# Multi-query attention: a planned schedule gets a second open accumulation group, a delay for dependent VectorE steps, longer lag and filler matmuls

## The chip, the cores and the metric

The kernel runs on one core of a Trainium2 chip. The metric is device time in microseconds (us) of that core. "Before" and "changed" are timed in alternating rounds on the same chip. Ratios are the mean time of one kernel's fast runs over that of the other's fast runs of the same rounds, so they are not quite the ratio of the medians quoted.

Names: TensorE (PE in the profile) multiplies matrices, ScalarE (ACT) computes the exponentials, VectorE (DVE) does elementwise work, SP issues transfers.

## The reference

```python
# q: (8, 1024, 16, 64), k and v: (8, 1024, 64), float32; one k and v for all 16 heads
scores  = np.matmul(q, k.T) / np.sqrt(64)        # per batch and head
weights = np.exp(scores - max); weights /= weights.sum(-1)
out     = np.matmul(weights, v)                  # (8, 1024, 16, 64)
```

## The kernel before

Two heads form a pair; there are 64 pairs, each with 8 tiles of 128 keys. For each tile TensorE computes scores in two halves ("qk", two matmuls each), and the exponential of a half goes to ScalarE ("act"). 77 of the 512 tiles are not exponentiated by ScalarE: VectorE copies their scores out ("z", twice) and makes the exponential from six elementwise steps. Then TensorE adds the weights up over the 8 tiles of a pair in three groups ("av"): group 0 sums the rows (weights of ones, 32 columns each), groups 1 and 2 multiply with v. VectorE evacuates each group ("ev"); a transposing transfer and a normalisation ("rec", "norm") follow.

The order of all this is not left to a scheduler. A function `plan` simulates TensorE, ScalarE and VectorE with fixed durations and writes a list of operations; each engine then executes its part of the list strictly in that order, waiting where data is not there yet.

```python
ACT_P, ACT_L = 0.905, 1.19                     # the plan's durations, us
QK_P, AV_P, SWITCH, PE_L = 0.22, 0.217, 0.10, 0.49
VEC = dict(z=1.13, ev=0.6, rec=0.22, norm=1.13)
STEPS = (0.6, 0.6, 0.6, 1.13, 1.13, 1.13)
TURN = 9.0                                     # evacuation to normalisation
BACKLOG, WBUFS, LAG = 4.5, 22, 1.4             # (three lines in the kernel)

def plan(NP, NKT):
    ...
    p, g, left = 0, 0, set(range(NKT))         # the one open group: pair, group, tiles left
    while p < NP:
        if pe <= dve:                          # TensorE's next operation
            ...
            # VectorE takes a tile where its work in hand is below BACKLOG
            if not vunits and nt < NT - NKT and todo < BACKLOG: ...
            ...                                # rs[j]: when tile j of the open group is ready
            j = min(rs, key=lambda j: (rs[j], j))
            tav = max(rs[j], acc[nacc % 2] if len(left) == NKT else 0.0)
            lag = min(LAG, 0.35 + (2 * NT - nq) / (6 * NKT))
            av = tav <= T + (SWITCH if mode != "av" else 0) and (
                nv < 3 * NKT * (nq / (2 * NKT) - lag) or nq == 2 * NT)
            ...
        else:                                  # VectorE's next operation, in this preference:
            ...                                # z, ev, rec/norm, then the steps of the oldest tile
            elif steps:
                t, n = steps.pop(0)
                emit(T, "step", t, n)
                dve = T + STEPS[n]
```

The lag keeps the value work some pairs behind the scores, so that TensorE has a stock of it; it shrinks towards the end. In the changed kernel `BACKLOG`, `WBUFS` and `LAG` become 5.0, 28 and 1.8.

The softmax here doesn't subtract the row's maximum and nothing guards it: scores larger than these inputs give would overflow.

## Time and profile before

| | before |
|---|---|
| time, median of 5 runs | 835.91 us (835.71 to 839.54) |
| span of the profiled run | 833.3 us |
| first exponential starts / last one starts | 9.19 / 818.57 us |
| median distance of two exponentials' starts | 904 ns |
| sum of the 869 distances above 904 ns ("excess") | 23.8 us |
| last exponential's start to the end ("tail") | 14.7 us |
| half-clock stretches before the last exponential | 9, together 51.2 us |

The excess, worked out from the instruction records: ScalarE is the fullest engine, it needs 904 ns per exponential, and what the distances add above that is time lost. Start + 869 x 904 ns + excess + tail gives the span.

The page of the kernel before: the span, each engine's busy time, the granted TensorE clock in 40 slices (tenths of full speed), and two groups by line with count, busy time, mean duration and the idle time before them.

```profile
span 833.3 us, 15240 instructions
...
PE 760.8 (91%) x6172; PEld 238.5 (29%) x6172; DVE 796.5 (96%) x943; ACT 803.1 (96%) x873; POOL 76.4 (9%) x91
...
PEclk8898999899999999999999999999999999999989
...
L339 ACT ACTIVATE wt<-sc 128x1024 f16<-128x1024 f32 x870 | 800.7, 1230 | 9.7 <-PE sc L327 9.6
L327 PE MATMUL sc<-qt,k2t 64*128 64x512 f16 x2048 | 364.1, 393 | 50.8 <-ACT wt L339 40.2
```

Two engines are 96% busy, and several slices show a clock of 8 tenths. The waits of the kernel before (who waited for whom, us in total, times, longest):

```profile
PE sc L327 <- ACT wt L339: 40.2, 112, 0.5
...
ACT wt L339 <- PE sc L327: 9.6, 20, 0.9
...
PE acc L383 <- DVE wt L370: 7.8, 24, 0.8
...
PE sc L327 <- DVE z L350: 4.7, 8, 1.1
```

The first wait is harmless: scores are ahead of ScalarE. The other three are not: ScalarE waits for scores, TensorE waits for a finished VectorE tile, and TensorE waits for VectorE to empty a score buffer. The TensorE timeline of the kernel before, ahead of the half-clock stretch at 236.7 us (start, duration, what, number of matmuls, idle time before and its releaser):

```profile
232.98 0.40 PE L383 MATMUL acc<-wt,ones 128*32 128x512 f16 x4
233.31 0.39 PE L327 MATMUL sc<-qt,k2t 64*128 64x512 f16 x2
234.13 0.39 PE L327 MATMUL sc<-qt,k2t 64*128 64x512 f16 x2 [0.43 <-ACT wt L339]
235.05 0.39 PE L327 MATMUL sc<-qt,k2t 64*128 64x512 f16 x2 [0.52 <-ACT wt L339]
236.37 1.18 PE L327 MATMUL sc<-qt,k2t 64*128 64x512 f16 x6 [0.92 <-DVE z L350]
237.50 0.62 PE L383 MATMUL acc<-wt,ones 128*32 128x512 f16 x4
```

From 233.3 to 237.5 us TensorE has score work only, though it has value work of later groups to do: the one open group lacks a tile that VectorE is still making. VectorE's last step of that tile:

```profile
236.23 1.22 DVE L370 TENSOR_TENSOR wt<-z,g 128x2048 uint16<-128x2048 uint16 x1
```

It ends at about 237.45 us, and the row-sum step that reads the tile starts at 237.50. The group of four row-sum matmuls takes 0.40 us at 232.98 and 0.62 us at 237.50: the clock has halved in between (the clock records show 0.50 for 3.4 us from 236.70 us).

### The profile page before, as it was taken

What the parts mean: (1) busy time and instruction counts of PE and PEld (TensorE: products, weight loads), DVE (VectorE), ACT (ScalarE), POOL (GpSimd) and SP (SyncE); (2) the same over time, 40 slices, a digit from 0 to 9 for tenths busy, and PEclk for the clock granted to TensorE, in tenths of its full rate; (3) what the DMA queues carried; (4) which work ended last, traced back from release to release, by engine and by line L of the source; (5) the groups of instructions that cost most, each with busy time, mean ns of one, the idle gap of its engine ahead of it and who ended that gap; (6) DMA issues with size and microseconds to landing.
All of it is one profiled execution on the core that took longest, in us unless ns stands there. A gap on an engine that the chain in (4) does not pass through costs nothing. (4 is left out here: it accounts for less than half of the span.)

```text
span 833.3 us, 15240 instructions
## 1 busy us (share of the span) xinstructions
PE 760.8 (91%) x6172; PEld 238.5 (29%) x6172; DVE 796.5 (96%) x943; ACT 803.1 (96%) x873; POOL 76.4 (9%) x91
## 2 busy tenths in 40 slices
PE   4988999899989989989989989999999999999986
PEld 1222232223323323323323323323323323323322
DVE  6999999999999999999999999999999999999994
ACT  6999999999999999999999999999999999999993
POOL 5100011010110002000020000000001000000000
PEclk8898999899999999999999999999999999999989
DMA  9956697667986689776698686775787676764524
GB/s 151 94 97 106 117 148 115 117 106 117 153 133 97 119 121 136 125 132 92 117 155 106 122 137 109 123 127 96 126 138 108 122 125 99 127 112 87 101 70 114
DMA packets 329846, 97.86 MB, mean 117 GB/s; under 512 B 263216, under 2 KB 329776, under 8 KB 329776
## 3 DMA queue, kind: packets, MB, share of 16 engines
q1 hardware_dynamic: 239792, 76.70, 47.1%
q0 software_dynamic: 88400, 19.40, 26.3%
q8 instruction: 48, 0.79, 0.4%
q10 hardware_dynamic: 1584, 0.79, 0.3%
q14 instruction: 22, 0.18, 0.1%
HBM read 39.58 MB, written 33.55 MB: 88 GB/s over the span
## 5 line engine op out<-in xcount | busy, mean ns | idle before, releaser
L339 ACT ACTIVATE wt<-sc 128x1024 f16<-128x1024 f32 x870 | 800.7, 1230 | 9.7 <-PE sc L327 9.6
L327 PE MATMUL sc<-qt,k2t 64*128 64x512 f16 x2048 | 364.1, 393 | 50.8 <-ACT wt L339 40.2
L391 PE MATMUL acc<-wt,v 128*64 128x512 f16 x2048 | 304.5, 393 | 0.0
L350 DVE TENSOR_SCALAR z<-sc 128x1024 uint16<-128x1024 f32 x154 | 187.6, 1218 | 10.2 <-PE sc L327 9.1
L327 PEld LDWEIGHTS <-k2t 64*128 64x128 f16 x2048 | 102.7, 94 | 323.2 <-issue 314.5
L383 PE MATMUL acc<-wt,ones 128*32 128x512 f16 x2048 | 167.7, 390 | 7.8 <-DVE wt L370 7.8
L399 DVE CAST ots<-acc 128x512 f16<-128x512 f32 x192 | 130.5, 679 | 10.2 <-PE acc L391 8.6
L391 PEld LDWEIGHTS <-v 128*64 128x64 f16 x2048 | 90.7, 109 | 152.9 <-issue 120.6
L275 POOL DMA_DIRECT2D qn<-in_q_dram x63 | 56.4, 895 | 638.0 <-DMA qt<-qn 637.6
L370 DVE TENSOR_TENSOR wt<-z,g 128x2048 uint16<-128x2048 uint16 x77 | 93.8, 1218 | 1.3 <-ACT wt L339 0.5
L369 DVE TENSOR_TENSOR g<-m,g 128x2048 f16<-128x2048 f16 x77 | 93.9, 1219 | 1.2
L368 DVE TENSOR_TENSOR m<-f,m 128x2048 f16<-128x2048 uint16 x77 | 93.7, 1217 | 0.0
L421 DVE TENSOR_TENSOR osb<-otq,rec 128x1024 f32<-128x1024 f16 x63 | 76.9, 1221 | 1.4
L383 PEld LDWEIGHTS <-ones 128*32 128x32 f16 x2048 | 42.8, 94 | 103.9 <-issue 96.7
L364 DVE TENSOR_SCALAR m<-f 128x2048 f16<-128x2048 uint16 x77 | 54.2, 704 | 2.2
L366 DVE TENSOR_SCALAR g<-f 128x2048 f16<-128x2048 uint16 x77 | 53.0, 689 | 0.0
L362 DVE TENSOR_SCALAR f<-z 128x2048 uint16<-128x2048 uint16 x77 | 52.8, 686 | 0.2
L412 DVE RECIPROCAL rec<-otq 128x16 f32<-128x16 f16 x63 | 15.3, 243 | 0.0
L253 POOL DMA_DIRECT2D k<-in_k_dram x14 | 12.5, 897 | 10.9 <-DMA k2t<-k 10.1
L260 POOL DMA_DIRECT2D v<-in_v_dram x8 | 7.0, 880 | 8.4 <-PE acc L391 7.3
L315 PE MATMUL kps<-ident,k 128*128 128x128 f16 x8 | 1.0, 308 | 5.9 <-DVE k L304 5.9
L320 ACT COPY qt<-qps 128x512 f16<-128x512 f16 x2 | 1.2, 586 | 4.8 <-PE qps L318 4.8
(18 smaller groups left out, 10.8 us busy)
## 6 DMA issues: line engine op xcount, KB each, us to landing
out_dram<-osb SPq DMA_DIRECT2D x63, 512.0 KB, 4.1
qn<-in_q_dram POOLq DMA_DIRECT2D x63, 256.0 KB, 4.6
k<-in_k_dram POOLq DMA_DIRECT2D x14, 128.0 KB, 5.5
v<-in_v_dram POOLq DMA_DIRECT2D x8, 128.0 KB, 6.2
qt<-qn SPq DMA_TRANSPOSE x63, 3.1
otq<-ots SPq DMA_TRANSPOSE x63, 4.8
qf<-in_q_dram ACTq DMA_DIRECT2D x2, 256.0 KB, 4.5
kn<-in_k_dram SPq DMA_DIRECT2D x1, 256.0 KB, 4.1
```

Source lines behind the costliest of these rows:

```text
L275: nc.gpsimd.dma_start(out=qn[p], in_=q[b, :, 2 * hp : 2 * hp + 2, :].rearrange("(c p) h d -> p c (h d)", p=P),)
L327: nc.tensor.matmul(sc[t, c][:, h, :], kst[p // HP]["k2t"][64 * h : 64 * h + 64, j, :], qt[p].rearrange("p c x -> p (c x)")[64 * h : 64 * h ...
L339: nc.scalar.activation(out=wt[t][:, :, c * QC : (c + 1) * QC], in_=sc.pop((t, c)), func=EXP, scale=ascale)
L350: nc.vector.tensor_scalar(out=z[:, :, c * QC : (c + 1) * QC], in0=sc.pop((t, c)), scalar1=vscale, scalar2=15 * ONE, op0=ALU.mult, op1=ALU.add,
L364: lambda: V.tensor_scalar(out=m, in0=f, scalar1=-ONE, scalar2=1.0 / ONE, op0=ALU.add, op1=ALU.mult),
L368: lambda: V.tensor_tensor(out=m, in0=f, in1=m, op=ALU.mult),
L369: lambda: V.tensor_tensor(out=g, in0=m, in1=g, op=ALU.mult),
L370: lambda: V.tensor_tensor(out=w.bitcast(U16), in0=z, in1=g, op=ALU.add),
L383: nc.tensor.matmul(a[32 * g : 32 * g + 32, :], ones16, w[:, h, cq * QC : (cq + 1) * QC], start=(n == 0), stop=(n == NKT - 1), tile_positio ...
L391: nc.tensor.matmul(a[64 * h : 64 * h + 64, :], vt[:, j, :], w[:, h, cq * QC : (cq + 1) * QC], start=(n == 0), stop=(n == NKT - 1), tile_po ...
L399: nc.vector.tensor_copy(out=ots[p][:, grp, :], in_=acc.pop((p, grp)))
L421: nc.vector.tensor_tensor(out=osb.rearrange("p i (h d) -> p (i h) d", h=2), in0=otq.pop(p)[:, 4:12, :].rearrange("p i (h d) -> p (i h) d", ...
```

## The change

Its intent, as far as the diff shows it: keep TensorE supplied, so that neither it nor its clock ever falls behind ScalarE. The core of the diff:

```diff
+VEC_DEP = 0.12
-BACKLOG = 4.5
-WBUFS = 22
-LAG = 1.4
+BACKLOG = 5.0
+WBUFS = 28
+LAG = 1.8
+def follows(x, y):     # does VectorE operation x read what y has just written?
...
-    while p < NP:
+    while p < NP or groups:
...
+            while len(groups) < 2 and p < NP:          # two open groups
+                a = 0 if all(x[3] for x in groups) else 1
+                groups.append((p, g, set(range(NKT)), a))
...              # the tile that is ready first, of the older group where one is ready
-            e = [x for x in evs if x[0] <= T]
-            f = [x for x in fin if x[0] <= T]
+            todo = [("ev", x) for x in evs if x[0] <= T]
+            todo += [("fin", x) for x in fin if x[0] <= T][:1]
+            todo += [("step", x) for x in steps if ...][:2]   # steps of two tiles
+            free = [x for x in todo if not follows(x[1], last)]
+            late = VEC_DEP if not free else 0.0
+            what, x = (free or todo or [("", None)])[0]
...
+        if len(run) >= 20 and True:                    # long runs of scores get fillers
+            idle.update(run[:-1])
...
+        for _ in range(10):                            # before the first transposes
+            for g in range(4):
+                nc.tensor.matmul(cold[32 * g : 32 * g + 32, :], ones16, wide, ...)
         turn_first()
...
+                if i in idle:
+                    fill(args[0] // NKT, 1)            # four matmuls into a free bank
```

`VEC_DEP` is what the trace of the kernel before shows: a VectorE step that reads what the step just before it wrote starts 1249 ns after that step, an independent one 1133 ns (719 against 600 ns for the shorter steps).

Besides, VectorE's buffer `g` is dropped (the weights tile holds that value) and `z` gets a third buffer, the first loads share the output buffers' pool, v is loaded two pairs later, and pair 62 is normalised ahead of the last evacuation instead of at the very end.

More of the change, by code (lines that the diff above doesn't have):

```diff
@@ L32 @@
 VEC_L = 0.19
+VEC_DEP = 0.12
 TURN = 9.0
-BACKLOG = 4.5
-WBUFS = 22
-LAG = 1.4
+BACKLOG = 5.0
+WBUFS = 28
+LAG = 1.8
 FAR = 1e9
+def follows(x, y):
+    if y is None or len(x) != len(y) and y[0] != "z":
+        return False
+    if len(x) == 3:
+        return x[1] == "norm" and y[1] == "rec" and x[2] == y[2]
+    if len(x) != 2:
+        return False
+    if y[0] == "z":
+        return x == (y[1], 0)
+    return x[0] == y[0] and (x[1], y[1]) in ((1, 0), (2, 0), (3, 1), (4, 3), (5, 4))
 def plan(NP, NKT):
@@ L54, in plan @@
     acc = [0.0] * 2
-    nacc = nq = nv = 0
+    nq = nv = 0
     nt, units, vunits = 0, [], []
@@ L61, in plan @@
     used = [0] * NT
-    p, g, left = 0, 0, set(range(NKT))
+    p, g = 0, 0
+    groups: list = []
     zs: list = []
@@ L66, in plan @@
     steps: list = []
-    while p < NP:
+    last = None
+    while p < NP or groups:
         if pe <= dve:
@@ L89, in plan @@
                 kind = "act"
-            rs = {}
-            for j in left:
-                t = NKT * p + j
-                if t in vtiles:
-                    rs[j] = ready.get(t, FAR)
-                elif g == 0:
-                    rs[j] = max(ready.get((t, 0), FAR), ready.get((t, 1), FAR))
-                else:
-                    rs[j] = ready.get((t, g - 1), FAR)
-            j = min(rs, key=lambda j: (rs[j], j))
-            tav = max(rs[j], acc[nacc % 2] if len(left) == NKT else 0.0)
+            while len(groups) < 2 and p < NP:
+                a = 0 if all(x[3] for x in groups) else 1
+                groups.append((p, g, set(range(NKT)), a))
+                g = (g + 1) % 3
+                p += g == 0
+            tav, pick = FAR, None
+            for grp in groups:
+                gp, gg, left, a = grp
+                for j in left:
+                    t = NKT * gp + j
+                    if t in vtiles:
+                        r = ready.get(t, FAR)
+                    elif gg == 0:
+                        r = max(ready.get((t, 0), FAR), ready.get((t, 1), FAR))
+                    else:
+                        r = ready.get((t, gg - 1), FAR)
+                    if len(left) == NKT:
+                        r = max(r, acc[a])
+                    if r < tav and (tav > T or grp is groups[0]):
+                        tav, pick = r, (grp, j)
             lag = min(LAG, 0.35 + (2 * NT - nq) / (6 * NKT))
@@ L139, in plan @@
                 nv += 1
-                emit(st, "av", p, g, j, NKT - len(left), nacc % 2)
-                left.discard(j)
-                used[NKT * p + j] += 1
-                if not left:
-                    acc[nacc % 2] = FAR
-                    evs.append((st + PE_L, p, g, nacc % 2))
-                    nacc += 1
-                    left = set(range(NKT))
-                    g = (g + 1) % 3
-                    p += g == 0
+                grp, j = pick
+                gp, gg, left, a = grp
+                emit(st, "av", gp, gg, j, NKT - len(left), a)
+                left.remove(j)
+                used[NKT * gp + j] += 1
+                if not left:
+                    acc[a] = FAR
+                    evs.append((st + PE_L, gp, gg, a))
+                    groups.remove(grp)
             else:
@@ L155, in plan @@
             z = [x for x in zs if x[0] <= T + 0.25]
-            e = [x for x in evs if x[0] <= T]
-            f = [x for x in fin if x[0] <= T]
+            todo = [("ev", x) for x in evs if x[0] <= T]
+            todo += [("fin", x) for x in fin if x[0] <= T][:1]
+            todo += [("step", x) for x in steps if x == min(y for y in steps if y[0] == x[0])][:2]
+            free = [x for x in todo if not follows(x[1], last)]
+            late = VEC_DEP if not free else 0.0
+            what, x = (free or todo or [("", None)])[0]
             if z:
-                zs.remove(z[0])
-                r, s, u = z[0]
+                x = z[0]
+                zs.remove(x)
+                r, s, u = x
                 T = max(T, r)
@@ L166, in plan @@
                     steps += [(u[0], n) for n in range(len(STEPS))]
-            elif e:
-                evs.remove(e[0])
-                _, ep, eg, a = e[0]
+                last = ("z", u[0])
+            elif what == "ev":
+                evs.remove(x)
+                _, ep, eg, a = x
                 emit(T, "ev", ep, eg, a)
@@ L174, in plan @@
                     fin += [(dve + VEC_L + TURN, k, ep) for k in ("rec", "norm")]
-            elif f:
-                fin.remove(f[0])
-                emit(T, f[0][1], ep := f[0][2])
-                dve = T + VEC[f[0][1]]
-            elif steps:
-                t, n = steps.pop(0)
-                emit(T, "step", t, n)
-                dve = T + STEPS[n]
-                if n == len(STEPS) - 1:
-                    ready[t] = dve + VEC_L
+                last = None
+            elif what == "fin":
+                fin.remove(x)
+                emit(T + late, *x[1:])
+                dve = T + late + VEC[x[1]]
+                last = x
+            elif what == "step":
+                steps.remove(x)
+                emit(T + late, "step", *x)
+                dve = T + late + STEPS[x[1]]
+                if x[1] == len(STEPS) - 1:
+                    ready[x[0]] = dve + VEC_L
+                last = x
             else:
@@ L187, in plan @@
                 dve = max(min(nxt, default=0.0), T + 1e-3)
+                last = None
+    for k, ep in [(k, ep) for _, k, ep in fin]:
+        emit(dve, k, ep)
     for _, ep, eg, a in evs:
         emit(dve, "ev", ep, eg, a)
-    for k, ep in [(k, ep) for _, k, ep in fin] + [("rec", NP - 1), ("norm", NP - 1)]:
+    for k, ep in [("rec", NP - 1), ("norm", NP - 1)]:
         emit(dve, k, ep)
@@ L220 @@
     qtp = ctx.enter_context(tc.tile_pool(name="qtp", bufs=3))
-    firstp = ctx.enter_context(tc.tile_pool(name="firstp", bufs=1))
     wtp = ctx.enter_context(tc.tile_pool(name="wtp", bufs=WBUFS))
@@ L233 @@
     nc.vector.memset(ones16, 1.0)
+    wide = consts.tile([P, QC], FP16, name="wide")
+    nc.vector.memset(wide, 0.0)
     kst: dict = {}
@@ L290, in load_first @@
         st = kst.setdefault(0, {})
-        st["kn"] = firstp.tile([P, NKT, D], FP32, name="kn")
+        st["kn"] = osbp.tile([P, NKT, D], FP32, tag="osb", name="kn")
         nc.sync.dma_start(out=st["kn"], in_=k[0].rearrange("(c p) d -> p c d", p=P))
-        st["qf"] = firstp.tile([P, NKT, 2 * D], FP32, name="qf")
+        st["qf"] = osbp.tile([P, NKT, 2 * D], FP32, tag="osb", name="qf")
         for c in range(NQC):
@@ L347, in exp_dve @@
         if c == 0:
-            zs[t] = dvp.tile([P, 2, S], U16, tag="z", name=f"z{name}")
+            zs[t] = dvp.tile([P, 2, S], U16, tag="z", bufs=3, name=f"z{name}")
         z = zs[t]
@@ L355, in exp_dve, with new @@
             return
-        f = dvp.tile([P, 2, S], U16, tag="f", name=f"f{name}")
-        m = dvp.tile([P, 2, S], FP16, tag="m", name=f"m{name}")
-        g = dvp.tile([P, 2, S], FP16, tag="g", name=f"g{name}")
         w = wt[t]
         V = nc.vector
+        x: dict = {}
+        def new(key, dtype):
+            x[key] = dvp.tile([P, 2, S], dtype, tag=key, name=f"{key}{name}")
+            return x[key]
         steps[t] = (
             lambda: V.tensor_scalar(
-                out=f, in0=z, scalar1=1023, scalar2=None, op0=ALU.bitwise_and),
+                out=new("f", U16), in0=z, scalar1=1023, scalar2=None, op0=ALU.bitwise_and),
             lambda: V.tensor_scalar(
-                out=m, in0=f, scalar1=-ONE, scalar2=1.0 / ONE, op0=ALU.add, op1=ALU.mult),
+                out=new("m", FP16), in0=x["f"], scalar1=-ONE, scalar2=1.0 / ONE,
+                op0=ALU.add, op1=ALU.mult),
             lambda: V.tensor_scalar(
-                out=g, in0=f, scalar1=GB / ONE, scalar2=GA, op0=ALU.mult, op1=ALU.add),
-            lambda: V.tensor_tensor(out=m, in0=f, in1=m, op=ALU.mult),
-            lambda: V.tensor_tensor(out=g, in0=m, in1=g, op=ALU.mult),
-            lambda: V.tensor_tensor(out=w.bitcast(U16), in0=z, in1=g, op=ALU.add),
+                out=w, in0=x["f"], scalar1=GB / ONE, scalar2=GA,
+                op0=ALU.mult, op1=ALU.add),
+            lambda: V.tensor_tensor(out=x["m"], in0=x["f"], in1=x["m"], op=ALU.mult),
+            lambda: V.tensor_tensor(out=w, in0=x["m"], in1=w, op=ALU.mult),
+            lambda: V.tensor_tensor(out=w.bitcast(U16), in0=z, in1=w, op=ALU.add),
         )
@@ L463, in finish_last, with fill @@
             )
+    filler = 0
+    def fill(p, n):
+        nonlocal filler
+        if len(open_acc) > 1:
+            return
+        s = 1 - open_acc[0] if open_acc else 0
+        filler += 1
+        d = psp.tile([P, QC], FP32, tag=f"acc{s}", name=f"fill{filler}")
+        for _ in range(n):
+            for g in range(4):
+                nc.tensor.matmul(
+                    d[32 * g : 32 * g + 32, :], ones16, qt[p].rearrange("p c x -> p (c x)")[:, 0:QC],
+                    start=True, stop=True, tile_position=(0, 32 * g),
+                )
+    open_acc: list = []
+    ops = plan(NP, NKT)[0]
+    idle: set = set()
+    run: list = []
+    for i, op in [(i, x[2]) for i, x in enumerate(ops) if x[2][0] in ("qk", "av")]:
+        if op[0] == "qk":
+            run.append(i)
+            continue
+        if len(run) >= 20 and True:
+            idle.update(run[:-1])
+        run = []
     begun = 0
@@ L473, in begin @@
                 load_k(b + 1)
+            if hp == 4:
                 load_v(b + 1)
@@ L483 @@
     with tc.manual_schedule(engines={ENG.PE, ENG.Activation, ENG.DVE}):
+        cold = psp.tile([P, QC], FP32, tag="sc0", name="cold")
+        for _ in range(10):
+            for g in range(4):
+                nc.tensor.matmul(
+                    cold[32 * g : 32 * g + 32, :], ones16, wide,
+                    start=True, stop=True, tile_position=(0, 32 * g),
+                )
         turn_first()
-        for _, _, (op, *args) in plan(NP, NKT)[0]:
+        for i, (_, _, (op, *args)) in enumerate(ops):
             if op == "qk":
@@ L497 @@
             elif op == "av":
+                if args[3] == 0:
+                    open_acc.append(args[4])
                 value(*args)
             elif op == "ev":
+                open_acc.remove(args[2])
                 evacuate(*args[:2])
```

## The prediction

> **What bounds it now.** ScalarE. The groups by line show 870 exponentials (800.7 us busy, 96%). In the instruction records their median start-to-start distance is 904 ns, so 869 distances need 785.6 us; they take 809.4 us, from 9.2 us (first start) to 818.6 us (last start). 23.8 us of ScalarE stalls lie inside, 9.2 us before and about 14 us after (span 833.3). VectorE is as full (796.5 us, 96%), TensorE has gaps of 60 us in sum.
>
> **Where the 23.8 us lie.** The clock records show half clock (0.50) in nine stretches of 3.4 to 13.7 us before the end (at 15, 46, 73, 148, 237, 363, 551, 677 and 800 us). Near them ScalarE loses 1.2 to 2.3 us each, 15.0 us together; the other 755 distances lose 8.8 us. In the timeline before each half-clock stretch TensorE does nothing but score matmuls, one pair (0.39 us) per exponential, because the single open accumulation group waits for a tile that VectorE has not finished[...]. [...]the stretches are multiples of 3.413 us.
>
> **What the change does.** Same work: 870 exponentials, 77 tiles by VectorE, 1536 value steps.
> - Two accumulation groups open, longer lag, 28 weight buffers: TensorE finds other value work when a tile is late. In the built order, runs of 4 or more score steps without a value step fall from 25 to 3 (the first run is 29, then one 6, one 4). That should remove the half-clock stretches after the head.
> - VectorE order: a dependent step right after its producer starts about 0.12 us later than an independent one (1249 against 1133 ns, 719 against 600). Such pairs fall from 164 to 45: about 14 us (estimate) less for VectorE. It is not the last limit, so this gives slack, not time, apart from score buffers freed sooner.
> - 40 warm-up matmuls before the first transposes, and 112 filler matmuls between the first scores, should keep the clock full in the head (at 15 to 28 us it was 0.50, 2.3 us lost). They run where TensorE is idle. First exponential 0.5 to 0.8 us earlier.
> - Cost: value/score switches rise from 1217 to 1483 (about 0.1 us each, 27 us by estimate). TensorE's gaps have room, but some scores may come later.
> - Tail: 35 instead of 30 value steps after the last score (5 x 0.217 = +1.1 us); but the second-last pair is normalised before the last evacuation instead of after everything, so the last output transfer starts about 2 us earlier. Net about -0.8 us.
>
> **Sum (estimates).** Half-clock losses 15.0 to about 1.5: -13.5. Other stalls 8.8 to about 6: -2.8. Head -0.8, tail -0.8. Together -17.9: **818 us** (-2.1%), range **811 to 826**. Floor if all stalls went: about 810. Chances: faster 0.57, same 0.41, slower 0.02.
>
> **What would show it.** Clock records: at most two half-clock stretches before the end, mean clock above 0.985 (0.968 now). Exponentials: start-to-start median still 904 ns, excess 5 to 11 us instead of 23.8; first start at 8.3 to 8.8 us. Waits: score matmuls after ScalarE persist, value matmuls waiting for VectorE's tile vanish (7.8 us now). VectorE busy nearly unchanged or 10 us lower, its idle time higher. TensorE gaps shorter.
>
> **What would make it wrong.** [...]more switches delay scores so that the 8.8 us grows, leaving 822 to 826 (within 2%); fillers delay the first scores; the late normalisation holds up the last evacuation. If the remaining excess goes to 3 us, 814.

The sum: -13.5 - 2.8 - 0.8 - 0.8 = -17.9 us, from the 835.91 us of the kernel before to 818 us. What the trace of the kernel before shows: in the 3.413 us ahead of each of the nine stretches TensorE is 36 to 63% busy. But from 297, 423, 485, 611 and 737 us on it is 47 to 48% busy for as long, and no half clock is recorded there. So when the clock halves is not shown; that more work for TensorE keeps it full was the assumption.

## The result, and the profile after

The changed kernel takes 822.05 us (median of 8 runs, 821.98 to 822.25) against 837.14 us (median of 15 runs, 835.71 to 839.70). The ratio is 0.982, with an interval of 0.9808 to 0.9832.

| | before | after | difference |
|---|---|---|---|
| span of the profiled run | 833.3 | 820.3 | -13.0 |
| first exponential starts | 9.19 | 8.45 | -0.74 |
| excess over 904 ns | 23.8 | 11.6 | -12.2 |
| tail | 14.7 | 14.7 | 0.0 |
| half-clock stretches before the last exponential | 9 | 0 | |
| spread of the timed runs | 4.0 | 0.3 | |

The page of the changed kernel:

```profile
span 820.3 us, 15521 instructions
...
PE 778.9 (95%) x6324; PEld 253.5 (31%) x6324; DVE 789.1 (96%) x944; ACT 800.5 (98%) x873; POOL 84.4 (10%) x91
...
PEclk9999999999999999999999999999999999999999
...
L378 ACT ACTIVATE wt<-sc 128x1024 f16<-128x1024 f32 x870 | 798.1, 1273 | 0.5 <-PE sc L366 0.3
L366 PE MATMUL sc<-qt,k2t 64*128 64x512 f16 x2048 | 367.2, 382 | 32.6 <-ACT wt L378 26.6
```

The clock is full (0.998 on average in this run, 0.968 before), and ScalarE's visible idle time falls from 9.7 to 0.5 us. (The excess is larger than the idle time, because an exponential's record runs past the start of the next one: 1273 ns long on average (1230 ns before), 904 ns apart. Of the changed kernel's 35 distances of 1000 to 1100 ns most still overlap, by 300 ns at the median, and only 4 of all 869 have no overlap left.) The waits of the changed kernel:

```profile
PE sc L366 <- ACT wt L378: 26.6, 94, 0.5
...
PE sc L366 <- DVE z L389: 1.4, 3, 0.7
...
ACT wt L378 <- PE sc L366: 0.3, 1, 0.3
```

TensorE's wait for a finished VectorE tile (7.8 us) is gone. The TensorE timeline of the changed kernel at the same time:

```profile
233.28 0.39 PE L366 MATMUL sc<-qt,k2t 64*128 64x512 f16 x2
233.60 0.62 PE L435 MATMUL acc<-wt,v 128*64 128x512 f16 x4
...
235.43 0.40 PE L427 MATMUL acc<-wt,ones 128*32 128x512 f16 x4
235.76 0.41 PE L435 MATMUL acc<-wt,v 128*64 128x512 f16 x2
```

Value matmuls stand between the scores, and at 235.43 a row-sum step and at 235.76 a value step of another group follow each other: two groups are open.

The tail did not move. VectorE's last operations before:

```profile
825.06 0.69 DVE L399 CAST ots<-acc 128x512 f16<-128x512 f32 x1 [1.04 <-PE acc L391]
...
826.01 1.29 DVE L452 TENSOR_TENSOR osb<-tr,rec 128x512 f32<-128x512 f16 x2
...
827.49 1.22 DVE L421 TENSOR_TENSOR osb<-otq,rec 128x1024 f32<-128x1024 f16 x1
```

and in the changed kernel:

```profile
810.70 1.22 DVE L465 TENSOR_TENSOR osb<-otq,rec 128x1024 f32<-128x1024 f16 x1
...
812.72 1.23 DVE L465 TENSOR_TENSOR osb<-otq,rec 128x1024 f32<-128x1024 f16 x1
813.86 0.68 DVE L443 CAST ots<-acc 128x512 f16<-128x512 f32 x1
...
814.80 1.29 DVE L496 TENSOR_TENSOR osb<-tr,rec 128x512 f32<-128x512 f16 x2
```

Pair 62's normalisation (812.72) has moved ahead of the last evacuation (813.86) as the prediction said. But the last exponential now starts at 805.62 and not 818.57 us: measured from there, the last evacuation comes at +8.24 us after the change and at +6.49 us before it (813.86 - 805.62 and 825.06 - 818.57). More value work is left over, and that eats what the earlier normalisation gives.

### The profile page after: what moved, and what is told of

Read it like the earlier page. It is cut to its first block, busy times and chain, and to the rows that moved or that the text cites. A ratio compares the mean times of both kernels' runs of the same rounds, so it can differ in the third digit from the quotient of the medians.

```text
span 820.3 us, 15521 instructions
## 1 busy us (share of the span) xinstructions
PE 778.9 (95%) x6324; PEld 253.5 (31%) x6324; DVE 789.1 (96%) x944; ACT 800.5 (98%) x873; POOL 84.4 (10%) x91
## 5 line engine op out<-in xcount | busy, mean ns | idle before, releaser
L378 ACT ACTIVATE wt<-sc 128x1024 f16<-128x1024 f32 x870 | 798.1, 1273 | 0.5 <-PE sc L366 0.3
L435 PE MATMUL acc<-wt,v 128*64 128x512 f16 x2048 | 326.4, 392 | 0.2 <-DVE ots L443 0.2
L366 PEld LDWEIGHTS <-k2t 64*128 64x128 f16 x2048 | 114.4, 93 | 302.9 <-issue 293.5
L389 DVE TENSOR_SCALAR z<-sc 128x1024 uint16<-128x1024 f32 x154 | 187.8, 1219 | 12.9 <-PE sc L366 10.1
L314 POOL DMA_DIRECT2D qn<-in_q_dram x63 | 64.3, 1020 | 618.7 <-DMA qt<-qn 618.3
L413 DVE TENSOR_TENSOR wt<-m,wt 128x2048 f16<-128x2048 f16 x77 | 93.7, 1217 | 0.8
L414 DVE TENSOR_TENSOR wt<-z,wt 128x2048 uint16<-128x2048 uint16 x77 | 92.6, 1203 | 0.4
L409 DVE TENSOR_SCALAR wt<-f 128x2048 f16<-128x2048 uint16 x77 | 56.3, 731 | 0.0
L521 PE MATMUL fill<-qt,ones 128*32 128x512 f16 x112 | 11.2, 390 | 0.0
L561 PE MATMUL cold<-wide,ones 128*32 128x512 f16 x40 | 4.1, 591 | 1.2 <-DVE wide L272 1.2
(23 smaller groups left out, 16.1 us busy)
```

The lines of the kernel that those rows point to most:

```text
L314: nc.gpsimd.dma_start(out=qn[p], in_=q[b, :, 2 * hp : 2 * hp + 2, :].rearrange("(c p) h d -> p c (h d)", p=P),)
L366: nc.tensor.matmul(sc[t, c][:, h, :], kst[p // HP]["k2t"][64 * h : 64 * h + 64, j, :], qt[p].rearrange("p c x -> p (c x)")[64 * h : 64 * h ...
L378: nc.scalar.activation(out=wt[t][:, :, c * QC : (c + 1) * QC], in_=sc.pop((t, c)), func=EXP, scale=ascale)
L389: nc.vector.tensor_scalar(out=z[:, :, c * QC : (c + 1) * QC], in0=sc.pop((t, c)), scalar1=vscale, scalar2=15 * ONE, op0=ALU.mult, op1=ALU.add,
L409: lambda: V.tensor_scalar(out=w, in0=x["f"], scalar1=GB / ONE, scalar2=GA, op0=ALU.mult, op1=ALU.add),
L413: lambda: V.tensor_tensor(out=w, in0=x["m"], in1=w, op=ALU.mult),
```

## The experiments

The first theory was the prediction's: **(1)** the half clock itself costs the 15 us that lie near its stretches. Rival 1: the late VectorE tile costs the time and the half clock is only its companion. Rival 2: VectorE's order is the gain. After four runs **theory 2** was formed: that VectorE is late against its planned time is a large part. Later it was given two readings: (2a) the VectorE time that the new order saves is what counts, (2b) the plan's knowledge of when VectorE is really done is what counts. All edits are to the kernel named; the medians of the kernel before in these rounds, on four chips, are 836.26 to 836.48 us.

| run | what | time, us | ratio | excess, us | half-clock stretches (us) | tail, us |
|---|---|---|---|---|---|---|
| | before | 837.14 | 1 | 23.8 | 9 (51.2) | 14.7 |
| | changed | 822.05 | 0.982 | 11.6 | 0 | 14.7 |
| b_head | before + head fillers | 834.90 | 0.9972 | 23.7 | 8 (37.5) | 14.7 |
| b_fill4 | before + fillers in all gaps | 828.52 | 0.9894 | 18.0 | 1 (3.4) | 14.9 |
| b_newlag | before + new constants | 831.05 | 0.9924 | 19.4 | 1 recorded (6.8) | 14.8 |
| a_nofill | changed - fillers | 823.44 | 0.9839 | 12.0 | none recorded | 14.7 |
| a_dveold | changed, old VectorE order | 827.40 | 0.9886 | 19.6 | 1 (6.8) | 12.6 |
| a_onegroup | changed, one group | 833.25 | 0.9958 | 24.6 | 8 (47.8) | 14.6 |
| a_oldlag | changed, old constants | 829.42 | 0.9918 | 17.5 | 5 (27.3) | 14.3 |
| a_dvemodel | changed, old order but delay counted | 821.44 | 0.9818 | 11.9 | 0 | 10.1 |
| a_switch | changed, group switch counted | 822.44 | 0.983 | 13.5 | 2 (6.8) | 13.7 |
| a_tail | changed, last pairs normalised early | 822.85 | 0.9835 | 11.9 | 0 | 15.3 |
| a_acttail | changed, last evacuations on ScalarE | 823.52 | 0.9848 | 13.3 | 2 (6.8) | 16.0 |
| a_lasttile | changed, no VectorE tile in the last two pairs | 820.52 | 0.9806 | 12.7 | 1 (3.4) | 10.6 |

Excess, stretches and tail are of the one profiled run of each. In `a_nofill` and `b_newlag` the head ran at the slow clock until about 32 us, which the clock records do not show (see below). "Near a stretch" means an exponential that starts from 4 us before it to 3.5 us after it.

### Does the half clock itself cost the time?

`b_head` is the kernel before with the warm-up and the fillers of the first long run of scores. `b_fill4` has the same warm-up and fillers in every run of four or more scores, and leaves the order of all real work as it was.

```diff
+        if len(run) >= 4:          # b_fill4;  b_head: >= 20
+            idle.update(run[:-1])
...
                 score(*args)
+                if i in idle:
+                    fill(args[0] // NKT, 1)
```

> The kernel before with the warm-up and the fillers of the first long run of scores only. Theory 1: the half clock at 15 us goes, the six to eight later stretches stay; about 3 us faster than before, 832 to 835 us, with the wide spread of before. Rivals 1 and 2: under 1.5 us faster (the first exponential 0.7 us earlier).

> The kernel before with its own order of real work, plus filler matmuls in the gaps of every run of 4 or more score steps and the warm-up at the start. Theory 1 (the half clock itself costs the time): the half-clock stretches vanish, the exponentials' excess over 904 ns falls from 23.8 to about 9 to 11 us, and the time falls to 820 to 824 us. Rival 1 (the late VectorE tile costs the time, the half clock is only its companion): clock full, but time still 833 to 837 us. Rival 2 (the gain of the change is VectorE's order): also 833 to 837 us.

Measured: 834.90 us (1.6 us under the median before, at the edge between the theories; its excess of 23.7 us is that of the kernel before) and 828.52 us, between the numbers of both. From `b_head` to `b_fill4` the half-clock time falls by 34.1 us and the kernel's time by 6.4 us, not by the 13 us that theory 1 asked for. The TensorE timeline of `b_fill4` where the kernel before stalled:

```profile
232.65 0.39 PE L329 MATMUL sc<-qt,k2t 64*128 64x512 f16 x2 [0.19 <-ACT wt L341]
232.97 0.40 PE L480 MATMUL fill<-qt,ones 128*32 128x512 f16 x4
233.97 0.39 PE L329 MATMUL sc<-qt,k2t 64*128 64x512 f16 x2 [0.60 <-DVE z L352]
234.29 0.40 PE L480 MATMUL fill<-qt,ones 128*32 128x512 f16 x4
```

The fillers keep the clock full here (0.40 us per four matmuls), but the score at 233.97 still waits 0.60 us for VectorE to empty its buffer. Two waits of `b_fill4`:

```profile
PE acc L385 <- DVE wt L372: 7.6, 16, 1.2
PE sc L329 <- DVE z L352: 6.2, 16, 1.6
```

Both waits for VectorE are there as before (7.8 and 4.7 us in the kernel before). Because both runs have the same order of exponentials, their distances can be set side by side: the 13.4 us of excess near the eight stretches of `b_head` are 5.3 us at the same exponentials of `b_fill4`, while the rest rises from 10.3 to 12.7 us (1.4 of these 2.4 us near the new stretch at 20.1 us). So the half clock cost about 8 us at its stretches and 6.4 us net of what the fillers themselves may cost, and a loss remains; that it is VectorE's lateness is suggested by these waits, not shown by them.

The head shows the same from the other side. `a_nofill` is the changed kernel without warm-up and fillers:

```diff
-        if len(run) >= 20 and True:
+        if False:
-        for _ in range(10):
+        for _ in range(0):
```

> The changed kernel without warm-up and fillers. Theory 1: half clock only in the first 30 us, time 824 to 826 us (3 us slower than the changed kernel, whose time is 822.05). Rivals 1 and 2: under 1.5 us slower than the changed kernel.

Measured: 823.44 us, 1.4 us slower, as the rivals said and not theory 1. The clock records show no half clock in this run before its end, but the timeline of `a_nofill` does:

```profile
26.05 0.61 PE L366 MATMUL sc<-qt,k2t 64*128 64x512 f16 x2 [0.31 <-ACT wt L378]
...
33.08 0.39 PE L366 MATMUL sc<-qt,k2t 64*128 64x512 f16 x2
```

A pair of score matmuls takes 0.61 us until about 32 us and 0.39 us from 33 us on: the slow clock of the head was simply not recorded. Running the head at it costs 0.74 us up to the first exponential (9.19 against 8.45 us; in the kernel before, which also starts at 9.19 us, the matmuls that turn k take 308 ns each, in the changed kernel 220 ns) and 0.4 us of excess after it. There is room for slow scores as long as they come in time.

### What do the constants do alone?

`b_newlag` changes nothing but the constants of the kernel before:

```diff
-BACKLOG = 4.5
-WBUFS = 22
-LAG = 1.4
+BACKLOG = 5.0
+WBUFS = 28
+LAG = 1.8
```

> The kernel before with the new constants alone (28 weight buffers, lag 1.8, backlog 5.0): one accumulation group, old VectorE order, no fillers. Runs of 4 or more scores fall from 25 to 2 (29 and 10). Theory 1: half clock in the head and perhaps at one later place, time 824 to 829 us. Rival 2 (VectorE's order is what gains): dependent VectorE pairs rise to 208, so 835 us or slower.

Measured: 831.05 us, again between the two. The recorded half clock is gone but for one stretch of 6.8 us, so behind the head the stock of value work alone feeds TensorE. (The head is as slow as in `a_nofill`, again without a record: a pair of score matmuls takes 0.61 us up to 31.5 us. Up to 40 us `b_newlag` has 1.8 us of excess, the changed kernel 1.3 us.) Yet the excess is 19.4 us, of which 2.1 us lie near that stretch. This, with `b_fill4`, is why theory 2 was formed: with the clock nearly full, 18 to 19 us of excess are left.

### Is it VectorE's order, or that the plan knows VectorE's time?

`a_dveold` takes VectorE's operations in the old order of preference; with that, the plan also no longer counts the 0.12 us of a dependent pair:

```diff
-            free = [x for x in todo if not follows(x[1], last)]
+            free = todo
```

> The changed kernel with VectorE's steps taken in the old order of preference (evacuation, normalisation, then the steps of the oldest tile in a row): 213 dependent pairs instead of 45, two groups, new constants, warm-up and fillers kept. If the half clock is what mattered (theory 1), it stays away and the time is 822 to 824 us. If VectorE being late against its planned time is the other half (theory 2, formed after the first four runs, where the clock was full and the exponentials still lost 18 to 19 us), the excess goes back to 16 to 20 us and the time to 827 to 831 us.

Measured: 827.40 us and an excess of 19.6 us, as theory 2 said. Its waits:

```profile
PE sc L366 <- DVE z L389: 10.1, 27, 0.7
ACT wt L378 <- PE sc L366: 4.2, 10, 1.2
```

TensorE waits 10.1 us, 27 times, for VectorE to empty score buffers (1.4 us, 3 times in the changed kernel), and ScalarE waits for those scores. This run does not yet tell the two readings of theory 2 apart, so `a_dvemodel` keeps the old order and only counts the delay. (Two small repairs were needed, because its last groups finish in another order.)

```diff
-            free = [x for x in todo if not follows(x[1], last)]
-            late = VEC_DEP if not free else 0.0
-            what, x = (free or todo or [("", None)])[0]
+            what, x = (todo or [("", None)])[0]
+            late = VEC_DEP if todo and follows(x, last) else 0.0
```

> The changed kernel with VectorE's steps in the old order of preference, but with the 0.12 us of each dependent pair now counted in the plan (173 dependent pairs; 75 tiles by VectorE, so 4 more exponentials = 3.6 us). Compared by the excess of the exponentials' distances over 904 ns, which does not depend on their number. If what counts is that the plan knows when VectorE is really done (theory 2b), the excess stays near 12 us and the time is 825 to 826.5 us (4 exponentials more). If what counts is the VectorE time saved by the order (theory 2a), the excess is 16 to 20 us as in the run with the old order, and the time 829 to 833 us.

Measured: an excess of 11.9 us, as reading 2b said. Its waits:

```profile
PE sc L365 <- DVE z L388: 0.8, 1, 0.8
...
ACT wt L377 <- PE sc L365: 0.3, 1, 0.3
```

With 173 dependent pairs, nearly as many as in the kernel before (164), the stalls are as small as in the changed kernel with its 45. So the new order is not needed to remove them; counting the delay is enough. How far VectorE runs behind its plan can be read by running each kernel's `plan` and setting it beside the trace (start of each score copy against its planned start, less what the exponentials themselves are behind by then): the mean is 0.34 us in `a_dveold`, -0.01 us in `a_dvemodel` and 0.07 us in the changed kernel. That fits reading 2b. But the plan that counts the delay also gives VectorE two tiles fewer. The busy times of `a_dveold` and of `a_dvemodel`:

```profile
PE 789.1 (96%) x6324; PEld 250.5 (30%) x6324; DVE 800.9 (97%) x944; ACT 803.4 (97%) x873; POOL 77.8 (9%) x91
...
PE 782.9 (96%) x6324; PEld 250.7 (31%) x6324; DVE 784.8 (96%) x928; ACT 804.0 (98%) x877; POOL 76.6 (9%) x91
```

VectorE is 16.1 us less busy with the delay counted, more than the 11.8 us that the new order saves (789.1 us in the changed kernel). That VectorE simply has less to do is therefore a rival that no run here excludes; the old order with the delay counted and 77 tiles would test it. The reordering does buy something else: 77 instead of 75 VectorE tiles, that is 4 exponentials or 3.6 us less for ScalarE. Even so, this run is not slower than the changed kernel (821.44 us), because its tail is 10.1 us instead of 14.7. That was not expected (825 to 826.5 us were), and is taken up below.

### Are two groups needed, and the constants?

`a_onegroup` opens one group at a time; `a_oldlag` restores the old constants.

```diff
-            while len(groups) < 2 and p < NP:
-                a = 0 if all(x[3] for x in groups) else 1
+            while len(groups) < 1 and p < NP:
+                a = nacc % 2
+                nacc += 1
```

> The changed kernel with one accumulation group open at a time (the two banks still take turns), VectorE order, constants, warm-up and fillers kept. Runs of 4 or more scores rise from 3 to 18. Theory 1: several half-clock stretches return and each costs about 1.6 us, so 828 us or more. Theory 2 (VectorE's lateness matters most, the half clock about 0.9 us each): some stretches return, time 824 to 828 us.

> The changed kernel with the old constants (22 weight buffers, lag 1.4, backlog 4.5), two groups, VectorE order, warm-up and fillers kept. 76 tiles by VectorE instead of 77, so two more exponentials (+1.8 us); dependent VectorE pairs 104; 7 runs of 4 or more scores. Both theories: 824 to 829 us; one or two half-clock stretches.

Measured: 833.25 and 829.42 us (the second slightly above what was expected, with five half-clock stretches instead of one or two). The first misses theory 2's 824 to 828 us and lies where theory 1 put it: the eight stretches and the stalls around them take 15.9 us together, 2 us each. One group brings the stall back in full; the TensorE timeline of `a_onegroup`:

```profile
323.39 0.39 PE L367 MATMUL sc<-qt,k2t 64*128 64x512 f16 x2 [0.53 <-ACT wt L379]
...
326.14 1.52 PE L367 MATMUL sc<-qt,k2t 64*128 64x512 f16 x6 [0.53 <-ACT wt L379]
```

Again TensorE has nothing but scores, and again the clock halves (at 326.1 us; a pair of score matmuls takes 0.39 us at 325.22 and 0.61 us at 327.97 us). The parts do not add up: taking one away costs 1.4 us (fillers), 5.4 us (order and counted delay), 7.4 us (constants) and 11.2 us (second group), together 25 us of a gain of 15 us (differences of the medians to 822.05 us). Each is worth its price only with the others: a second group with a plan that is wrong about VectorE leaves as much excess as the constants alone (19.6 us in `a_dveold`, 19.4 in `b_newlag`). Note that each edit of the plan changes the whole order of operations, so these are differences of schedules and not of single waits.

### Does the remaining excess come from uncounted switches of TensorE?

A step starts 0.22 to 0.24 us after one of its own kind, and 0.31 to 0.34 us after one of another kind, row-sum against value too (start-to-start medians in both kernels). The plan counts this between scores and values, not between row sums and values. `a_switch` counts it:

```diff
-            av = tav <= T + (SWITCH if mode != "av" else 0) and (
+            amode = "one" if pick and pick[0][1] == 0 else "av"
+            av = tav <= T + (SWITCH if mode != amode else 0) and (
```

> The changed kernel whose plan also counts 0.1 us where TensorE goes from a row-sum group (weights of 32 columns) to a value group or back; the trace shows such a step starting 0.33 us after the one before, against 0.22 within a group, and the plan left it out. If the remaining 11.6 us of excess come from score matmuls that are late because the plan thinks TensorE faster than it is, the excess falls to 8 to 10 us and the time to 818 to 821 us. If the excess comes from elsewhere, 822 us as the changed kernel.

Measured: 822.44 us, with runs from 821.19 to 823.49 us: no gain. Its excess of 13.5 us has 2.9 us near two half-clock stretches, so 10.6 us without them. Inconclusive; where the last 11.6 us of excess come from stays open. They are a departure from the plan: run by itself, the changed kernel's plan has only 0.4 us of such excess. What the records show of it is that 64 distances of the changed kernel are more than 60 ns too long, 8.0 us in sum, and that 20 of the 27 over 100 ns are two series of ten, of 194 to 195 and of 131 to 132 ns, each repeating every 62.3 us: a repeating place of the plan, not chance.

### What holds the tail?

`a_tail` normalises the last pairs 4 us after their evacuation instead of 9; `a_acttail` lets ScalarE evacuate the last pair and normalises only pair 61 early (5 us).

```diff
-  fin += [(dve + VEC_L + TURN, k, ep) for k in ("rec", "norm")]
+  fin += [(dve + VEC_L + (TURN if ep < NP - 4 else 4.0), k, ep) for k in ("rec", "norm")]   # a_tail
...
+        copy = nc.scalar.copy if p == NP - 1 else nc.vector.tensor_copy                     # a_acttail
```

> The changed kernel with the last four pairs normalised 4 us after their evacuation instead of 9 us. In the trace of the changed kernel the tail after the last exponential starts is as long as before (14.7 us), because the outputs of pairs 61 and 62 are normalised at 810.7 and 812.7 us and then queue ahead of the last pair's output in the DMA engines. If that is what holds the tail, it shortens by 1 to 2 us: 820 to 821 us. If the tail is held by the matmuls of the last pair, the time stays at 822.

> The changed kernel with the last pair evacuated by ScalarE, which is idle by then, and pair 61 alone normalised 5 us after its evacuation. The run with both pairs earlier made the tail 0.6 us longer because VectorE waited for the transposed pair 62 ahead of the last evacuation. With the last evacuation on another engine that wait holds up nothing, and the output of pair 61 no longer queues ahead of the last output: tail 13.2 to 14.2 us instead of 14.7, time 820.8 to 821.8 us. If the tail is set by the matmuls and the last transfers alone, 822.

The reason for trying: in the changed kernel the packets of the outputs of pairs 61 and 62 and of half of pair 63 run without a break from 812.86 to 817.78 us. Both missed: 822.85 and 823.52 us, with longer tails (15.3 and 16.0 us). In `a_tail` the break is there (SP issues the outputs of pairs 61 and 62 at 807.89 and 814.74 us), but VectorE waits 1.05 us for the transposed pair 62 ahead of the last evacuation, which starts only at 814.63 us. The second one shows why one cannot simply hurry. SP's transfers at the end of `a_acttail`:

```profile
810.04 0.37 SPq L473 DMA_DIRECT2D out_dram<-osb  x1
810.64 1.99 SPq L451 DMA_TRANSPOSE otq<-ots  x1
816.86 0.37 SPq L473 DMA_DIRECT2D out_dram<-osb  x1
```

Pair 61's output (512 KB) now goes out at 810.04 us, just ahead of the transposing transfer of pair 62. The packets of the transposition run from 812.77 to 814.83 us, after the output's (810.95 to 813.16 us), and VectorE waits 4.7 us for it. (Its body also met two half-clock stretches.)

`a_dvemodel` points elsewhere: only 13 value steps are left after its last score, 35 in the changed kernel, where 22 value and 32 row-sum and 32 value matmuls follow the last score (TensorE timeline of the changed kernel):

```profile
805.03 0.39 PE L366 MATMUL sc<-qt,k2t 64*128 64x512 f16 x2
805.35 2.56 PE L435 MATMUL acc<-wt,v 128*64 128x512 f16 x22
807.85 1.91 PE L427 MATMUL acc<-wt,ones 128*32 128x512 f16 x32
809.69 3.64 PE L435 MATMUL acc<-wt,v 128*64 128x512 f16 x32
```

The reading is that a VectorE tile near the end comes late and value work piles up behind it (that the tile is what holds it up is argued). `a_lasttile` gives VectorE no tile in the last two pairs (with the same two repairs as `a_dvemodel`):

```diff
-                if not vunits and nt < NT - NKT and todo < BACKLOG:
+                if not vunits and nt < NT - 2 * NKT and todo < BACKLOG:
```

> The changed kernel with no VectorE tile in the last two pairs instead of the last one (76 tiles by VectorE, so 2 more exponentials = +1.8 us; 18 instead of 35 value steps after the last score, 17 x 0.217 = -3.7 us; two small repairs of the plan's last evacuations that this needs). The run that counted the dependent pairs in the plan but did not reorder had a tail of 10.1 us against 14.7 with only 13 value steps left, and matched the changed kernel although it ran 4 more exponentials. If the value steps left over, held up by a late VectorE tile, are what holds the tail, the tail here is 10.5 to 11.5 us and the time 819.5 to 821 us. If the tail is held by the outputs' transfers, the tail stays above 13.5 us and the time is 823 to 824 us.

Measured: 820.52 us (820.10 to 821.36), tail 10.6 us, as expected of theory "value steps left over". In its profiled run the tail is 4.1 us shorter, for two more exponentials (1.8 us), 1.1 us more excess and 0.1 us less head, so a span 1.4 us shorter. Its ratio to before, 0.9806 (0.9786 to 0.9826), lies below the changed kernel's 0.982, but the intervals overlap, as the two were timed in different rounds; the gain over the changed kernel is some 0.2% by the medians and is not proven by the intervals. It is the fastest median.

## Why the prediction was right or wrong

The range (811 to 826 us) held the result, and the forecast of -17.9 us was near the measured -15.1 us (difference of the medians). Part of that nearness is luck: the profiled runs differ by 13.0 us, and the other 2.1 us are scatter of the kernel before. It leaned to "faster by over 2%" (0.57); the ratio of 0.982 is just within 2%. Point by point:

- **"Half-clock losses 15.0 to about 1.5: -13.5."** The outcome holds: no stretch is left, and the mean clock is 0.998. The reading behind it was wrong in size. The 15.0 us near the stretches are not all the clock's: with a filled clock and the same order (`b_fill4` against `b_head`) 6.4 us were gained, and 5.3 of 13.4 us stayed at the same exponentials. Low TensorE activity, the half clock and ScalarE's stall had, by the timeline at 233 to 237 us, one cause in common, TensorE held up by VectorE (it is 45% busy in the 3.4 us ahead of the half clock), and the prediction booked all to the clock.
- **"Other stalls 8.8 to about 6: -2.8."** This step failed. With no half clock anywhere, the whole excess is 11.6 us, 2.8 us more than the 8.8 us. The prediction itself named this risk ("so that the 8.8 us grows"). Why they are 11.6 us stays open; the one attempt (`a_switch`) did not lower the time.
- **"It is not the last limit, so this gives slack, not time"** (the VectorE order). This step failed in part. The order itself is indeed not needed to remove the stalls: `a_dvemodel` does without it. What the prediction missed is that the same lines tell the plan when VectorE is done, and that is worth time: without them the kernel takes 827.40 us, 5.4 us more. Whether the plan's knowledge counts or VectorE's lighter load that comes with it stays open.
- **Head -0.8:** -0.74, right. The further 2.3 us lost in the slow head were booked to the clock; without fillers the whole head costs only 1.4 us.
- **"Tail -0.8":** 0.0. The 5 more value steps were counted and the earlier normalisation happened, but the last evacuation came 1.75 us later after the last exponential (8.24 against 6.49 us): the value work lasted longer, and the evacuation had to wait behind the normalisation of pair 62 (from 812.72 us, for 1.23 us), while the last value matmul was done at 813.33 us. Of the 1.75 us, 1.26 us are later value work (its end comes 7.71 against 6.45 us after the last exponential's start) and 0.49 us that wait.
- **Signs in the profile:** the excess of 11.6 us lies just above the 5 to 11 us foreseen. The wait for VectorE's tile vanished (7.8 us to none), the start-to-start median stayed 904 ns, and TensorE's gaps fell from 60 to 35 us, as said. VectorE was 7.4 us less busy (796.5 to 789.1 us), as said; its idle time did not rise as foreseen, since the span shrank by 13.0 us.

So where did the gain come from? 0.7 us from the head, 12.2 us from the body, nothing from the tail (profiled runs); the rest of the 15.1 us is the scatter of the kernel before, whose timed runs spread over 4.0 us and whose profiled run (835.05 us) was faster than all of them. In the body, by the runs that take parts away, it came from value work at hand for TensorE (constants and second group) together with a plan that counts VectorE's delay.

## What to carry to other kernels

A schedule that is fixed in advance is only as good as the durations in it: a 0.12 us delay per dependent pair (1249 against 1133 ns from start to start), left out of the plan, cost 5 to 8 us (5.4 us of time, 7.7 us of excess), and counting it was enough here, at the price of two tiles fewer for VectorE. When a stall and a half clock stand side by side, fill the gaps with dummy matmuls in the same order: what that gains is the clock's share less what the fillers cost, and what remains has another cause (here 6.4 us were gained, and 5.3 of 13.4 us of excess remained). After a body has been tightened, count the work that is left over behind the last operation of the limiting engine, and take care of which transfers are queued ahead of the last ones.
